# First tile's shift from eight one-column matmuls, second tile and two weight slabs loaded in two parts, one split held behind a norm's first step

## The chip, the cores and the metric

The kernel runs on one core of a Trainium2 chip (trn2). The metric is the device time of one execution in microseconds (us), the median over several executions. A profile of one further execution records every instruction of every engine: TensorE as PE (matmuls) and PEld (weight loads), VectorE as DVE, ScalarE as ACT, GpSimd as POOL, and the queue of SyncE, which issues the transfers, as SPq.

## What is computed

Two layers, each with three sub-layers over 256 tokens of width 1024 (`x`), in 32-bit floats. Every sub-layer is fed `x * (1 + scale) + shift`, and its result enters a layer norm through a gate. The nine vectors of a layer come from one conditioning vector `c`.

```python
c_act = jax.nn.silu(c)
for l in range(DEPTH):
    mod = c_act @ mod_w[l] + mod_b[l]
    sh1, sc1, g1, sh2, sc2, g2, sh3, sc3, g3 = jnp.split(mod, N_MOD, axis=-1)
    f = swiglu(modulate(x, sh1, sc1), ffn_in[l, 0], ffn_out[l, 0])
    x = deepnorm_residual(x, f, g1, ln_g[l, 0], ln_b[l, 0], 0.5)
    u = modulate(x, sh2, sc2)
    m = even_mixer(u, ...) if l % 2 == 0 else odd_mixer(u, ...)
    x = deepnorm_residual(x, m, g2, ln_g[l, 1], ln_b[l, 1])
    f = swiglu(modulate(x, sh3, sc3), ffn_in[l, 1], ffn_out[l, 1])
    x = deepnorm_residual(x, f, g3, ln_g[l, 2], ln_b[l, 2], 0.5)
```

## The kernel before, in words

Activations lie transposed: eight tiles k = 0..7 of 128 features by 256 tokens. All weights are read once, in the order in which they are used, as slabs of 1 MiB (16 blocks of 128x128, `wst`). A slab is turned, half by half, into two parts that TensorE multiplies faster than plain 32-bit data: ACT rounds it (`whi`, line 365), DVE subtracts the rounded part from the raw one (`wlo`, line 374, called the split here). A product is then three matmuls (`mm3`, lines 489 to 491): high weight with high activation, high weight with low activation, low weight with high activation. Slab 0 alone is used raw, in plain 32-bit matmuls.

The columns of `mod` are made on DVE: line 450 multiplies a 128x1024 tile of transposed `mod_w` by silu(c), spread over all partitions (`cact`), and sums each row. That gives one column (one tile k, one of the nine vectors) per instruction. For the first tile, k = 0, the two columns (shift and scale) are made from halves of 512, as soon as each half of the spread vector is there: four instructions at line 468 (`reduce_first`).

The head runs like this. SP issues, in this order, `cvec` (c and the first biases), `m0a` and `m0b` (the rows of `mod_w` for tile 0, half by half, the second with tile 0 of x), slab 0, `m1x` (the rows of tile 1 with tiles 1 to 3 of x), slab 1, the rows of tile 2, slab 2, the rows of tile 3, slab 3, `x47` (the other tiles of x), `cols`, and then slabs and rows of `mod_w` in turn. TensorE runs five warming matmuls (line 524), four matmuls that spread silu(c) over the partitions (line 556), and seven further warming matmuls. Then the first pass of the first channel mixer begins: k = 0 to 3, with eight columns j of gate and up each (line 970), sixteen products for every k from slab k. Ahead of the products of k, `first_u(k)` queues on ACT and DVE, in an order that is fixed by hand (`queue_behind`): the two reductions of k, the halving of slab k's first half (ACT 365, DVE 374), the modulated tile (`uhi` at line 649, `ut` at line 651, `ulo` at line 657), then the second half of the slab. After k = 3 the eight sums are set aside (line 986) and the next columns follow with all k, now by `mm3`.

A channel mixer ends with eight output tiles f, each the sum over 22 products (`ffn_out`). `tile_out` (line 770 for the tile `yy`, line 777 for its square) adds the residual. After f = 7, `stats` lets TensorE sum the parts that came before (line 807), multiplies ahead for the next sub-layer (lines 489 to 491 on `flat`), sums the last tile (line 816) and its square (line 817), and goes on multiplying ahead. Conversions of weights run five half slabs ahead of their use, so a split stands in DVE's queue every eight products. With `W.defer` set, `conv_to` doesn't queue a split but keeps it in `W.pending`, and `tile_out` issues it right behind the next `yy`. The kernel before does that at the end of the odd mixer only.

Of the kernel before, what the change touches and what calls it, by code (L numbers as in the profile page):

```python
# [11 lines left out]
F32 = mybir.dt.float32  # L12
F32R = mybir.dt.float32r
BF16 = mybir.dt.bfloat16
# [7 lines left out]
P = 128  # L22
# [36 lines left out]
RAWSLABS = 1  # L59
NWARM = (5, 7)  # L60

# [180 lines left out]
@with_exitstack  # L242
def trunk_kernel(ctx: ExitStack, tc: tile.TileContext, cvec, m0a, m0b, m1x, x47, pos, wst, modw, colsd,
                 rgw, wa2, outT):
# [69 lines left out]
    class Stream:  # L314
# [22 lines left out]
        def dma_to(self, n):  # L337
            while self.ndma < min(n, NSLAB):
                s = self.ndma
                self.mods_to(self.mod_target(s))  # L340
                t = T(wraw, [P, SLAB * P], tag="wraw")
                self.raw[s] = t
                self.ndma += 1
                self.last_dma = sync.dma_start(t, wst[s])
                if s == KSPLIT - 1:
                    sync.dma_start(self.xrest, x47)
                    sync.dma_start(cols, colsd)
# [60 lines left out]
        def mods_to(self, n):  # L408
            while self.nmod < n:
                if self.nmod < KSPLIT:  # L410
                    t = self.early_mod(self.nmod)
                else:
                    t = T(wraw, [P, 2, DM], tag="wraw")
                    sync.dma_start(t, modw[self.nmod])
                self.todo += [(2 * self.nmod + q, t[:, q, :], self.ndma) for q in range(2)]
                self.nmod += 1

        def begin(self, first, second):

            a, b = (t.rearrange("p j s -> p (j s)") for t in (first, second))  # L420
            HD = DM // 2
            self.m0 = [[a[:, o + v * HD:o + (v + 1) * HD] for v in range(2)] for o in (0, DM)]
            self.m0rows = a[:, :DM], a[:, DM:2 * DM + SEQ]
            o = 2 * DM + SEQ
            self.m1rows = a[:, o:o + 2 * DM + (KSPLIT - 1) * SEQ]
            pair = lambda t: t.rearrange("p (v d) -> p v d", v=2)
            self.early = [None, pair(a[:, o:o + 2 * DM])] + [pair(b[:, i * 2 * DM:(i + 1) * 2 * DM]) for i in range(2)]
            x1 = o + 2 * DM
            self.xrest = b[:, 4 * DM:4 * DM + (KD - KSPLIT) * SEQ]
            self.x = [a[:, 2 * DM:2 * DM + SEQ]] + [a[:, x1 + i * SEQ:x1 + (i + 1) * SEQ] for i in range(KSPLIT - 1)] + \  # L430
                [self.xrest[:, i * SEQ:(i + 1) * SEQ] for i in range(KD - KSPLIT)]

        def early_mod(self, n):
            if n == 0:

                for t, m in zip(self.m0rows, (m0a, m0b)):
                    sync.dma_start(t, m)
                return self.m0rows[0].rearrange("p (v d) -> p v d", v=2)
            sync.dma_start(*((self.m1rows, m1x) if n == 1 else (self.early[n], modw[n])))
            return self.early[n]  # L440

# [16 lines left out]
        def reduce_first(self):  # L458

            part = T(const, [P, 2], tag="part")  # L460
            for v in (SH, SC):
                self.modcols[(0, v)] = T(const, [P, KD], tag=f"mod0_{v}")
            del self.todo[:2]
            for h in range(2):
                for v, t, b in zip((SH, SC), self.m0[h], (shb, scb)):
                    junk = T(wk, [P, DM], BF16, tag="junk", bufs=1)
                    p = part[:, v:v + 1]
                    i = vec.tensor_tensor_reduce(junk[:, :DM // 2], t, spread[h], float(P), b[:, 0:1] if h == 0 else p, MULT,
                                                 ADD, p if h == 0 else self.modcols[(0, v)][:, 0:1])
                    queue_behind(i, self.last_reduce)  # L470
                    self.last_reduce = i

# [59 lines left out]

    chi = T(const, [P, KD], F32R, tag="chi")
    clo = T(const, [P, KD], tag="clo")
    with tc.high_priority():
        ta(chi, cT, AF.Silu)
        ta(clo, cT, AF.Silu)
        vec.tensor_tensor(clo, clo, chi.bitcast(F32), SUB)
        dhi, dlo = (T(main, [P, KD, P], F32R, tag=f"flat{q}") for q in range(2))
# [19 lines left out]
        for i, j in zip(pds[1:], pds):  # L559
            queue_behind(i, j)  # L560

    warm(NWARM[1], pds[-1])

# [50 lines left out]
    def begin(first, second):  # L614
        W.begin(first, second)
        W.dma_to(1)

        W.last_reduce = vec.tensor_scalar(scb, scb, 1.0, None, ADD)
# [313 lines left out]
    def ffn(l, i, prev):  # L932
        with tc.tile_pool(name=nm("ffn"), bufs=1) as fp:
# [77 lines left out]
            for f in range(KD):  # L1011
                ps = mmps()
                for k in range(NJ):
                    mm3(ps[:, :SEQ], W.next((("ffn_out", l, i), k, f)), (hhi[:, k, :], hlo[:, k, :]),
                        k == 0, k == NJ - 1)
# [530 lines left out]
def _lay_out(inp):  # L1546
# [50 lines left out]
    xt = f["x"][0].T.reshape(KD, P, SEQ).transpose(1, 0, 2)  # L1597
    halves = modw[0].reshape(P, 2, 2, DM // 2).transpose(2, 0, 1, 3).reshape(2, P, DM)

# [10 lines left out]
    for i, name in enumerate(("rg_wa", "rg_wx")):  # L1610
        for n in range(2 * KD):
# [4 lines left out]
            [as_cols(f["c"])] + [as_cols(f["mod_b"][0, v * DM:(v + 1) * DM]) for v in (SH, SC)], axis=1)),  # L1616
        "m0a": beside(halves[0]),
        "m0b": beside(halves[1], xt[:, 0]),
        "m1x": beside(modw[1], xt[:, 1:KSPLIT]),
        "x47": beside(xt[:, KSPLIT:]),  # L1620
# [25 lines left out]
```

## Time and profile before

| | us |
|---|---|
| median of 3 runs | 1008.31 (1007.86 to 1008.39) |
| the profiled execution | 1007.84 |
| its span, first to last instruction | 1006.1 |
| PE busy in the span | 995.9 |
| DVE busy | 878.2 |
| ACT busy | 611.7 |
| mean granted clock of TensorE, as a share of full | 0.997 |

Matmuls are pipelined, so that a busy PE is not PE at its peak; what counts is where PE stands still or waits. "Idle before" in brackets at the end of a row is the time that the engine had stood still when the instruction began, and what ended it. Weight loads (PEld) run ahead of the matmuls that they belong to, and their starts show best when PE came free.

### The profile page before, as it was taken

Reading aid. Unit: us, or ns where it says so; the run is one execution under the profiler, and the core shown is the slowest. Engines: PE = TensorE matmul, PEld = TensorE weight load, DVE = VectorE, ACT = ScalarE, POOL = GpSimd, SP = SyncE. Lnnn points to the kernel's source line nnn. Section 1 sums busy time; section 2 is a strip of 40 time slices with the busy share of each in tenths; the row PEclk is TensorE's granted clock in tenths of the full one; section 3 lists DMA queues with packets and bytes.
Section 4 is the critical chain, followed back from the end, with each engine's and each line's share of the span. In section 5 each row is a group of like instructions: output and inputs, shape, how many; then the busy total and the mean of one; then the engine's idle time right before and its main releaser. Section 6 shows DMA issues by size and latency. Waiting matters only on the chain.

```text
span 1006.1 us, 20567 instructions
## 1 busy us (share of the span) xinstructions
PE 995.9 (99%) x8354; PEld 976.0 (97%) x8354; DVE 878.2 (87%) x1511; ACT 611.7 (61%) x1033; POOL 4.6 (0%) x24
## 2 busy tenths in 40 slices
PE   9999999999999999999999999999999999999997
PEld 8999999998999999999999999999999999999996
DVE  6789999998999899999996999999788799666664
ACT  4656655578886766645554665454568767554542
POOL 0000000000000000000000000000000000000000
PEclk9999999999999999999999999999999999999998
DMA  9998698755467744799975479898743156766501
GB/s 373 421 392 325 252 365 313 296 210 219 158 244 296 297 169 171 298 374 394 342 298 221 171 267 387 326 329 333 281 168 126 50 183 240 283 217 246 190 21 42
DMA packets 36383, 258.79 MB, mean 257 GB/s; under 512 B 4160, under 2 KB 4416, under 8 KB 5312
## 3 DMA queue, kind: packets, MB, share of 16 engines
q1 hardware_dynamic: 36144, 257.09, 67.8%
q8 instruction: 65, 1.06, 0.4%
q10 hardware_dynamic: 144, 0.39, 0.1%
q14 instruction: 30, 0.25, 0.1%
HBM read 256.42 MB, written 1.05 MB: 256 GB/s over the span
## 4 chain that ended last, share of the span: by engine, by line
PE 85%; DVE 8%; ACT 3%; issue 3%; DMA 1%; SPq 0%; DVEq 0%; ACTq 0%
PE mm L491 26%; PE mm L490 25%; PE mm L489 25%; DVE wlo L374 3%; DVE junk L450 2%; DMA wraw<-wst 1%; ACT whi L365 1%; PE mm L1267 1%; PE mm L1268 1%; PE mm L1266 1%; PE ax L490 1%; PE ax L491 1%; PE ax L489 1%; PE ax L1467 0%; PE mm L1441 0%
## 5 line engine op out<-in xcount | busy, mean ns | idle before, releaser
L374 DVE TENSOR_TENSOR wlo<-wraw,whi 128x1024 fp32r<-128x1024 f32 x338 | 408.7, 1217 | 72.6 <-ACT whi L365 71.9
L365 ACT ACTIVATE whi<-wraw 128x1024 fp32r<-128x1024 f32 x338 | 354.0, 1057 | 163.1 <-PE mm L490 117.2
L491 PE MATMUL mm<-uhi,wlo 128*128 128x256 f32 x1624 | 449.1, 277 | 0.2 <-DVE wlo L374 0.2
L489 PE MATMUL mm<-uhi,whi 128*128 128x256 f32 x1624 | 449.3, 277 | 0.0
L490 PE MATMUL mm<-ulo,whi 128*128 128x256 f32 x1624 | 449.1, 277 | 0.0
L491 PEld LDWEIGHTS mm<-uhi,wlo 128*128 128x128 f32 x1624 | 304.6, 188 | 0.7 <-DVE wlo L374 0.4
L489 PEld LDWEIGHTS mm<-uhi,whi 128*128 128x128 f32 x1624 | 304.8, 188 | 0.4 <-ACT uhi L1470 0.2
L490 PEld LDWEIGHTS mm<-ulo,whi 128*128 128x128 f32 x1624 | 304.8, 188 | 0.4
L489 PE MATMUL mm<-hhi,whi 128*128 128x256 f32 x704 | 194.4, 276 | 0.0
L491 PE MATMUL mm<-hhi,wlo 128*128 128x256 f32 x704 | 194.4, 276 | 0.0
L490 PE MATMUL mm<-hlo,whi 128*128 128x256 f32 x704 | 194.4, 276 | 0.0
L450 DVE CUSTOM_DVE_ANT_0 junk<-wraw,cact,cols 128x1024 bf16<-128x1024 f32 x128 | 163.1, 1275 | 4.8 <-DMA wraw<-modw 4.5
L490 PEld LDWEIGHTS mm<-hlo,whi 128*128 128x128 f32 x704 | 132.2, 188 | 0.0
L489 PEld LDWEIGHTS mm<-hhi,whi 128*128 128x128 f32 x704 | 132.2, 188 | 0.0
L491 PEld LDWEIGHTS mm<-hhi,wlo 128*128 128x128 f32 x704 | 132.2, 188 | 0.0
L565 ACT ACTIVATE hhi<-h 128x256 fp32r<-128x256 f32 x88 | 35.8, 413 | 66.4 <-DVE h L947 66.2
L777 ACT ACTIVATE ysq<-yy 128x256 f32<-128x256 f32 x42 | 17.5, 416 | 59.9 <-DVE yy L770 59.6
L947 DVE SCALAR_TENSOR_TENSOR h<-mm,sg 128x256 f32<-128x256 f32 x75 | 30.3, 414 | 6.4 <-PE mm L491 6.4
L566 DVE TENSOR_TENSOR hlo<-h,hhi 128x256 fp32r<-128x256 f32 x88 | 35.6, 414 | 0.1
L770 DVE SCALAR_TENSOR_TENSOR yy<-mm,gate,ax 128x256 f32<-128x256 f32 x48 | 22.9, 478 | 13.8 <-PE mm L491 13.7
L511 ACT ACTIVATE sg<-mm 128x256 f32<-128x256 f32 x75 | 27.4, 367 | 6.1 <-PE mm L491 3.0
L489 PE MATMUL mm<-flat,whi 128*128 128x258 f32 x96 | 28.5, 297 | 0.0
(340 smaller groups left out, 1126.9 us busy)
## 6 DMA issues: line engine op xcount, KB each, us to landing
wraw<-wst SPq DMA_DIRECT2D x170, 1024.0 KB, 5.6
wraw<-modw SPq DMA_DIRECT2D x68, 1024.0 KB, 6.6
hhi<-modw SPq DMA_DIRECT2D x2, 1024.0 KB, 16.1
hlo<-m1x SPq DMA_DIRECT2D x1, 1408.0 KB, 9.7
wraw<-rgw SPq DMA_DIRECT2D x1, 1024.0 KB, 5.5
hlo<-m0b SPq DMA_DIRECT2D x1, 640.0 KB, 4.7
hlo<-m0a SPq DMA_DIRECT2D x1, 512.0 KB, 3.6
hhi<-x SPq DMA_DIRECT2D x1, 512.0 KB, 20.9
```

Of the source, the lines that this page charges most:

```text
L365: ia = act.activation(hi, raw, AF.Copy)
L374: i = vec.tensor_tensor(lo, raw, hi.bitcast(F32), SUB)
L450: i = vec.tensor_tensor_reduce(junk, t, cact, 1.0, bias, MULT, ADD, self.modcols[(l, v)][:, j:j + 1])
L489: pe.matmul(ps, hi, mh, start=start, stop=False, skip_group_check=shared)
L490: pe.matmul(ps, hi, ml, start=False, stop=False, skip_group_check=shared)
L491: W.last_product = pe.matmul(ps, lo, mh, start=False, stop=stop, skip_group_check=shared)
L511: i = act.activation(out, in_, func, **kw)
L565: act.activation(hi, src, AF.Copy)
L566: return vec.tensor_tensor(lo, src, hi.bitcast(F32), SUB)
L770: i = vec.scalar_tensor_tensor(y, ps, self.gate[:, f:f + 1], ax[:, f, :], MULT, ADD)
L777: act.activation(ysq, y, AF.Square)
L947: vec.scalar_tensor_tensor(h, pu, bu, sg, ADD, MULT)
```

## The change

For tile 0, the shift isn't reduced on DVE any more. Its 128 columns of `mod_w` are loaded as eight blocks of 128x128, with as many bytes as before, and TensorE multiplies each by one column of silu(c) (a new tile `cs`), summing in PSUM; DVE then adds the bias. Line 468's four instructions become two, for the scale. The eight matmuls stand behind the spreading ones, and four warming matmuls follow instead of seven. `m1x` becomes two transfers: the first row set with tile 1 of x, then the second row set with tiles 2 and 3. Slabs 1 and 2 are each loaded by two transfers, half by half. At the end of the first channel mixer, from the twelfth product of the last output tile on, `W.defer` is set.

```diff
-NWARM = (5, 7)
+NWARM = (5, 4)
...
-                self.last_dma = sync.dma_start(t, wst[s])
+
+                parts = 2 if RAWSLABS <= s < RAWSLABS + 2 else 1
+                for q in range(parts):
+                    n1 = SLAB * P // parts
+                    self.last_dma = sync.dma_start(t[:, q * n1:(q + 1) * n1], wst[s][:, q * n1:(q + 1) * n1])
...
-            self.m0 = [[a[:, o + v * HD:o + (v + 1) * HD] for v in range(2)] for o in (0, DM)]
+
+            self.m0 = a[:, :HD], a[:, DM:DM + HD]
+            self.m0shift = [a[:, o + k * P:o + (k + 1) * P] for o in (HD, DM + HD) for k in range(KD // 2)]
...
-            self.m1rows = a[:, o:o + 2 * DM + (KSPLIT - 1) * SEQ]
+            o2 = o + DM + SEQ
+            end = o2 + DM + (KSPLIT - 2) * SEQ
+
+            self.m1rows = a[:, o:o2], a[:, o2:end]
...
-            sync.dma_start(*((self.m1rows, m1x) if n == 1 else (self.early[n], modw[n])))
-            return self.early[n]
+                return [None, None]
+            if n == 1:
+                for t, m in zip(self.m1rows, (m1a, m1b)):
+                    sync.dma_start(t, m)
+                return self.early[1]
+            sync.dma_start(self.early[n], modw[n])
+            return [self.early[n][:, q, :] for q in range(2)]
...
-            for h in range(2):
-                for v, t, b in zip((SH, SC), self.m0[h], (shb, scb)):
-                    junk = T(wk, [P, DM], BF16, tag="junk", bufs=1)
-                    p = part[:, v:v + 1]
-                    i = vec.tensor_tensor_reduce(junk[:, :DM // 2], t, spread[h], float(P), b[:, 0:1] if h == 0 else p, MULT,
-                                                 ADD, p if h == 0 else self.modcols[(0, v)][:, 0:1])
-                    queue_behind(i, self.last_reduce)
-                    self.last_reduce = i
+            scale, shift = (self.modcols[(0, v)][:, 0:1] for v in (SC, SH))
+            for h, t in enumerate(self.m0):
+                junk = T(wk, [P, DM], BF16, tag="junk", bufs=1)
+                i = vec.tensor_tensor_reduce(junk[:, :DM // 2], t, spread[h], float(P), part if h else scb[:, 0:1], MULT, ADD,
+                                             scale if h else part)
+                queue_behind(i, self.last_reduce)
+                self.last_reduce = i
+            i = vec.tensor_tensor(shift, self.shift0, shb[:, 0:1], ADD)
+            queue_behind(i, self.last_reduce)
+            self.last_reduce = i
...
+    cs = T(const, [P, KD], tag="cs")
...
-        ta(clo, cT, AF.Silu)
-        vec.tensor_tensor(clo, clo, chi.bitcast(F32), SUB)
+        ta(cs, cT, AF.Silu)
+        vec.tensor_tensor(clo, cs, chi.bitcast(F32), SUB)
...
-    warm(NWARM[1], pds[-1])
...
         W.dma_to(1)
+
+        sp = mmps()
+        W.shift0 = sp[:, 0:1]
+        prods = [pe.matmul(sp[:, 0:1], w, cs[:, k:k + 1], start=k == 0, stop=k == KD - 1) for k, w in enumerate(W.m0shift)]
+        after = pds[-1]
+        for i in prods:
+            queue_behind(i, after)
+            after = i
+        warm(NWARM[1], after)
...
                 for k in range(NJ):
+                    if l == 0 and i == 0 and f == KD - 1 and k == NJ // 2:
+
+                        W.defer = True
```

## Rows read from the trace of the kernel before

**Rows 1.** Page, busy time of each engine over the span.
```profile
PE 995.9 (99%) x8354; PEld 976.0 (97%) x8354; DVE 878.2 (87%) x1511; ACT 611.7 (61%) x1033; POOL 4.6 (0%) x24
```
**Rows 2.** Waits of the whole span: engine, line, releaser, us in total, times, longest.
```profile
PEld mm L970 <- ACT uhi L649: 1.2, 3, 0.5
```
**Rows 3.** Chain that ended last, 0 to 30 us: start, us, what.
```profile
3.19 11.62 DMA wraw<-wst
```
**Rows 4.** Timeline, TensorE in the head: start, us, engine, line, operation, count, idle before.
```profile
5.87 2.52 PE L524 MATMUL mm<-ones_dm 128*128 128x128 f32 x14
9.17 5.45 PE L970 MATMUL mm<-ut,wraw 128*128 128x256 f32 x24 [0.78 <-ACT ut L651]
16.43 1.00 PEld L970 LDWEIGHTS mm<-uhi,whi 128*128 128x128 f32 x8 [0.49 <-ACT uhi L649]
...
28.17 0.99 PEld L970 LDWEIGHTS mm<-uhi,whi 128*128 128x128 f32 x8 [0.34 <-ACT uhi L649]
33.63 0.19 PEld L489 LDWEIGHTS mm<-uhi,whi 128*128 128x128 f32 x1
```
**Rows 5.** Timeline, ACT and DVE in the head.
```profile
4.72 0.17 DVE L618 TENSOR_SCALAR cfirst<-cfirst 128x8 f32<-128x8 f32 x1
8.52 0.60 ACT L651 ACTIVATE ut<-hlo,mod,mod 128x256 f32<-128x256 f32 x1 [4.15 <-DVE mod L468]
12.48 1.28 DVE L450 CUSTOM_DVE_ANT_0 junk<-hlo,cact,cfirst 128x1024 bf16<-128x1024 f32 x1 [2.46 <-DMA hlo<-m1x]
14.83 1.06 ACT L365 ACTIVATE whi<-wraw 128x1024 fp32r<-128x1024 f32 x1 [3.99 <-DMA wraw<-wst]
26.11 1.06 ACT L365 ACTIVATE whi<-wraw 128x1024 fp32r<-128x1024 f32 x1 [2.11 <-DMA wraw<-wst]
27.52 0.60 ACT L649 ACTIVATE uhi<-hlo,mod,mod 128x256 fp32r<-128x256 f32 x1 [0.35 <-DVE mod L450]
```
**Rows 6.** Timeline, SP's queue: rows of tile 3, slab 3 and `x47` issued.
```profile
4.86 0.51 SPq L439 DMA_DIRECT2D hhi<-modw  x1
5.42 0.44 SPq L344 DMA_DIRECT2D wraw<-wst  x1
6.46 0.33 SPq L346 DMA_DIRECT2D hhi<-x  x1
```
**Rows 7.** DMA issues, the same three: KB, us from issue to landing.
```profile
hhi<-modw SPq DMA_DIRECT2D x1, 1024.0 KB, 18.9
wraw<-wst SPq DMA_DIRECT2D x1, 1024.0 KB, 20.7
hhi<-x SPq DMA_DIRECT2D x1, 512.0 KB, 20.9
```
**Rows 8.** Waits of SP's queue, 0 to 60 us.
```profile
SPq L346 <- DMA hlo<-m0b: 0.6, 1, 0.6
```
**Rows 9.** Windows: us; busy PE, PEld, DVE, ACT, POOL; granted clock; DMA share; GB/s.
```profile
5.00:10.00 5.00, 4.22 (x21) 3.74 (x20) 3.42 (x9) 1.45 (x4) 0.00 (x0) 1.00 1.03 431
```
**Rows 10.** Chain that ended last: 16 plain 32-bit products of 64 columns (two entries each).
```profile
275.02 3.52 PE mm L1216 x32
```
**Rows 11.** Timeline, first norm: DVE and TensorE.
```profile
191.93 1.22 DVE L374 TENSOR_TENSOR wlo<-wraw,whi 128x1024 fp32r<-128x1024 f32 x1
192.18 0.54 PEld L807 LDWEIGHTS ax<-early,ones_d 128*128 128x128 f32 x4
193.06 0.48 DVE L770 SCALAR_TENSOR_TENSOR yy<-mm,gate,ax 128x256 f32<-128x256 f32 x1
194.43 0.19 PEld L489 LDWEIGHTS mm<-flat,whi 128*128 128x128 f32 x1
194.49 0.48 DVE L741 SCALAR_TENSOR_TENSOR flat<-yy,A,flat 128x256 fp32r<-128x256 f32 x1 [0.94 <-ACT flat L740]
```
**Rows 12.** Timeline, norm after the second layer's first mixer: TensorE.
```profile
737.29 0.54 PEld L807 LDWEIGHTS ax<-early,ones_d 128*128 128x128 f32 x4
738.97 0.19 PEld L489 LDWEIGHTS mm<-flat,whi 128*128 128x128 f32 x1
```

More of the change, by code (lines that the diff above doesn't have):

```diff
@@ L242, in trunk_kernel @@
 @with_exitstack
-def trunk_kernel(ctx: ExitStack, tc: tile.TileContext, cvec, m0a, m0b, m1x, x47, pos, wst, modw, colsd,
+def trunk_kernel(ctx: ExitStack, tc: tile.TileContext, cvec, m0a, m0b, m1a, m1b, x47, pos, wst, modw, colsd,
                  rgw, wa2, outT):
@@ L414, in mods_to @@
                     sync.dma_start(t, modw[self.nmod])
-                self.todo += [(2 * self.nmod + q, t[:, q, :], self.ndma) for q in range(2)]
+                    t = [t[:, q, :] for q in range(2)]
+                self.todo += [(2 * self.nmod + q, t[q], self.ndma) for q in range(2)]
                 self.nmod += 1
@@ L421, in begin @@
             HD = DM // 2
-            self.m0 = [[a[:, o + v * HD:o + (v + 1) * HD] for v in range(2)] for o in (0, DM)]
+            self.m0 = a[:, :HD], a[:, DM:DM + HD]
+            self.m0shift = [a[:, o + k * P:o + (k + 1) * P] for o in (HD, DM + HD) for k in range(KD // 2)]
             self.m0rows = a[:, :DM], a[:, DM:2 * DM + SEQ]
             o = 2 * DM + SEQ
-            self.m1rows = a[:, o:o + 2 * DM + (KSPLIT - 1) * SEQ]
+            o2 = o + DM + SEQ
+            end = o2 + DM + (KSPLIT - 2) * SEQ
+            self.m1rows = a[:, o:o2], a[:, o2:end]
             pair = lambda t: t.rearrange("p (v d) -> p v d", v=2)
-            self.early = [None, pair(a[:, o:o + 2 * DM])] + [pair(b[:, i * 2 * DM:(i + 1) * 2 * DM]) for i in range(2)]
-            x1 = o + 2 * DM
+            self.early = [None, (a[:, o:o + DM], a[:, o2:o2 + DM])] + [pair(b[:, i * 2 * DM:(i + 1) * 2 * DM]) for i in range(2)]
             self.xrest = b[:, 4 * DM:4 * DM + (KD - KSPLIT) * SEQ]
-            self.x = [a[:, 2 * DM:2 * DM + SEQ]] + [a[:, x1 + i * SEQ:x1 + (i + 1) * SEQ] for i in range(KSPLIT - 1)] + \
+            self.x = [a[:, 2 * DM:2 * DM + SEQ], a[:, o + DM:o2]] + \
+                [a[:, o2 + DM + i * SEQ:o2 + DM + (i + 1) * SEQ] for i in range(KSPLIT - 2)] + \
                 [self.xrest[:, i * SEQ:(i + 1) * SEQ] for i in range(KD - KSPLIT)]
@@ L437, in early_mod @@
                     sync.dma_start(t, m)
-                return self.m0rows[0].rearrange("p (v d) -> p v d", v=2)
-            sync.dma_start(*((self.m1rows, m1x) if n == 1 else (self.early[n], modw[n])))
-            return self.early[n]
+                return [None, None]
[5 more added lines that the diff above has]
+            return [self.early[n][:, q, :] for q in range(2)]
         def reduce(self):
@@ L458, in reduce_first @@
         def reduce_first(self):
-            part = T(const, [P, 2], tag="part")
+            part = T(const, [P, 1], tag="part")
             for v in (SH, SC):
@@ L1597, in _lay_out @@
     xt = f["x"][0].T.reshape(KD, P, SEQ).transpose(1, 0, 2)
-    halves = modw[0].reshape(P, 2, 2, DM // 2).transpose(2, 0, 1, 3).reshape(2, P, DM)
+    HD = DM // 2
+    shift0 = f["mod_w"][0][:, SH * DM:SH * DM + P].reshape(KD, P, P).transpose(1, 0, 2).reshape(P, DM)
     def beside(*a):
@@ L1616, in _lay_out @@
             [as_cols(f["c"])] + [as_cols(f["mod_b"][0, v * DM:(v + 1) * DM]) for v in (SH, SC)], axis=1)),
-        "m0a": beside(halves[0]),
-        "m0b": beside(halves[1], xt[:, 0]),
-        "m1x": beside(modw[1], xt[:, 1:KSPLIT]),
+        "m0a": beside(modw[0][:, SC, :HD], shift0[:, :HD]),
+        "m0b": beside(modw[0][:, SC, HD:], shift0[:, HD:], xt[:, 0]),
+        "m1a": beside(modw[1][:, 0], xt[:, 1]),
+        "m1b": beside(modw[1][:, 1], xt[:, 2:KSPLIT]),
         "x47": beside(xt[:, KSPLIT:]),
```

## The prediction

> **What bounds the kernel now.** I read the page first: TensorE is busy for 99% of the span [rows 1], so the end moves only where TensorE stands still. The list of waits then names the places that the change could touch: three waits of the first pass, 1.2 us together, for the modulated tile `uhi` [rows 2]. The timeline shows where they lie, and what a norm waits for.
>
> In the head, TensorE's first real product begins at 9.17, and the sixteen products of k = 1, 2, 3 follow. Their starts at 16.43 and 28.17 stood idle for ACT's `uhi` [rows 4]. From 28.17 to 33.63 there is no wait inside, so sixteen halved products cost TensorE 5.46 us. For k = 0 the products are plain: 24 entries in 5.45 us, less some 0.17 of overlap at the end, make 0.22 us each, and 32 of them some 7.0 us [rows 4].
>
> What `uhi` waits for is told by ACT and DVE. ACT's conversion of slab 1 waited for the slab until 14.83, that of slab 3 until 26.11; the first reduction of tile 1 waited for `m1x` until 12.48 [rows 5]. The chain of the first 30 us is, for its first 15 us, one transfer, slab 1's [rows 3]. So the head is bound by arrival, and the DMA engines are full there (share 1.03, 431 GB/s [rows 9]): what lands can be used in smaller pieces, but not brought sooner as a whole.
>
> At the first norm, DVE begins a split at 191.93; `yy` stands behind it and starts at 193.06, although TensorE had begun loading for the sums, which follow its last product, at 192.18. TensorE is back on product work at 194.43 [rows 11].
>
> **The change part by part.** *First tile.* Two of four DVE reductions go. Before, their end let ACT start `ut` at 8.52, and with 0.60 us of that, TensorE began at 9.17 [rows 4, 5]. Now the shift comes from eight plain products, sixteen entries, behind the spreading ones at 5.87. The trace has no one-column product. The nearest rows: 64 columns take 3.52/32 = 0.11 us an entry [rows 10]; the warming ones in the same place take 2.52/14 = 0.18 [rows 4]. So the products take 1.8 to 2.9 us and end at 7.6 to 8.8; fewer columns may cut it further, but the weights must be loaded all the same, so I set no lower end than 0.11. I take 8.5, nearer to the warming rows, which stand in the same microseconds. With 0.17 for the addition [rows 5], some 0.1 of signals and `ut`'s 0.65 to the first product, TensorE starts at 9.4 to 9.5: 0.3 later, not earlier (bounds 9.0, where the earlier end leads after slab 0 is in, and 9.8). The four warming matmuls (eight entries, 0.9 to 1.4 us) stand ahead of the first product in TensorE's queue and end at 9.4 to 9.9, and may push it as far as 9.9. DVE is freed for 0.75 us or so, with nothing waiting there.
>
> *Tile 1 and slabs 1 and 2 in two parts.* Bytes and order stay, so a first half lands half a transfer earlier. From slab 3 to `x47`, half a slab took 6.46 + 20.9 - 5.42 - 20.7 = 1.24 us [rows 6, 7]; so slab 1's first half lands at about 13.6 instead of 14.8, and tile 1's first rows about 1.9 before 12.4. Both reductions of tile 1 are then done by 13.8, ACT has the half slab converted by 14.7 and `uhi` 0.6 later, before TensorE leaves k = 0 at 9.5 + 7.0 = 16.5. That start no longer waits. Tile 2 follows. In the trace its products began at about 22.3 (16.43 + 5.46, and a third of the 1.2 us of waiting [rows 2]); its reductions stand behind tile 1's splits on DVE and move up by the same microsecond, so it can begin at 21.3. TensorE arrives at 16.5 + 5.46 = 21.96. No wait.
>
> Tile 3 is what is late next. Slab 3 isn't split, and lands at 26.1 as before; ACT's fixed order puts `uhi` behind that conversion: 26.11 + 1.06 = 27.15 or so, with the start overlapping, and 0.65 more (27.52 to 28.17) to the product: 27.8 [rows 4, 5]. The reductions must also be done: the rows of tile 3 land at 4.86 + 18.9 = 23.8 [rows 6, 7], and two reductions of 1.3 from there end at 26.4, ahead of 27.15 instead of behind the conversion at 27.5. TensorE itself arrives at 21.96 + 5.46 = 27.4. So k = 3 begins at 27.8 instead of 28.17: **0.4 us gained**, whatever the first tile does, as long as TensorE's first product starts before 27.8 - 2 x 5.46 - 7.0 = 9.9. The bounds: 0 if TensorE starts k = 0 at 10.2 or slab 3 lands 0.4 later, 0.8 if slab 3 lands early (then TensorE's own 27.4 decides).
>
> The queues that the parts pass: SP issues three transfers more. `x47` was held until `m0b` had landed, eight transfers before it [rows 8], so I read a limit of eight in flight. Three more in the row put slab 3's issue back from 5.42 to where the first part of tile 1 lands, about 10.5. There are then seven transfers, 4.75 MiB, ahead of it, some 11 us of work at the full rate, so the engines don't run dry. `x47` and `cols` go behind as before.
>
> A rule of the Trainium skill speaks against this part. "DMA: Bandwidth & Descriptors" (section Measured) wants transfers of 1 MiB or more, and its anatomy section gives a fixed cost of about 2 us for each. By that, three more transfers would put slab 3 off by up to 6 us. The row above disagrees: the half-size `x47` landed 1.24 us behind the slab ahead of it, with no fixed cost.
>
> *The held split.* The last output tile's conversions come at every eighth product; the channel mixer has 352 products of the first kind and 22 for each output, so the last one begins at 506, `W.defer` is set at 517, and one boundary, 520, lies behind it before 528. So exactly the split of 191.93 is held. Its price is read from a norm of the same kind in which nothing stood in DVE's way: there TensorE took from 737.29 to 738.97, 1.68 us, between the same two steps that took 192.18 to 194.43, 2.25 us, here [rows 11, 12]. **0.57 us gained.** The split (1.22) now lies between `yy` and the steps on DVE that follow the sums. In the trace DVE stood idle for 0.94 us there, waiting for ACT, until 194.49 [rows 11]; the split fills that and puts off what follows by 0.1 to 0.3, against 0.6 by which `yy` is earlier. The weights that it makes are wanted some 3 us later. Bounds: 0 (some other step of DVE takes its place) and 0.8.
>
> **Does the gain last?** Behind 33.6 the same steps follow from TensorE's progress, and every transfer issued there is released by a buffer that DVE frees. DVE is busy for 87% of the span [rows 1], but its work starts from buffers that TensorE frees, so it moves with it. I count nothing for that and nothing gained.
>
> **The sum.** 0.4 + 0.57 = 0.97 us off the profiled execution's 1007.84: 1006.87. The median of the runs stands 0.47 above that execution, so the forecast for the median is 1007.3, which is 0.1% less than 1008.31. A difference of 0.2%, 2.0 us, is about what a measurement can tell from no change.
>
> **The rivals.** *Only the norm gains* (chance 0.2): slab 3 lands 0.4 later, or the first product comes after 9.9 because of the warming matmuls. 1008.31 - 0.57 = 1007.7. *Slab 3 lands earlier* by a microsecond, as transfers in parts are spread better (0.12): 0.8 + 0.6, 1006.9 and down to 1006.5 with both upper bounds. *The hold does nothing* (0.06): DVE has something else ahead of `yy`: 1007.9.
>
> *TensorE's clock* (0.06, slower): the granted clock reads 1.00, the level of 2.4 GHz, in 5 to 10 us [rows 9], but the entries tell another story, 0.18 us for 128 columns in the warming matmuls against 0.11 later for 64 [rows 4, 10], so TensorE seems to be at the lower level until the last of them. Sixteen entries of one column in their place keep the array nearly empty. If the higher level comes later for that, plain products of k = 0 cost 0.44 instead of 0.22. From 1.4 us of such delay on, six or seven entries, the gains are gone; with half of k = 0, 3.5 us more, k = 3 begins at 9.5 + 10.5 + 10.9 = 30.9, 2.7 later: 1008.31 + 2.7 - 0.57 = 1010.4; with all of it 1014. For it: nothing but these eight products changes there. Against it: loads and matmuls still follow without a gap. "TensorE: Matmul & The Clock Gate" of the Trainium skill (Part 1) has the same: throttled is the default, and activity releases it. By that rule, if one-column products count for little, the loss is as above; no run shows it yet.
>
> *The order of work elsewhere moves* (0.06, mostly slower): the added tile and the hold shift what the planner places, and DVE, with 13% of its time free [rows 1], delays a norm: a stall of the 0.6 us of the first norm at three of the other five, 1.7 us, or as much gained. *More transfers cost* (0.02): slab 3 some 6 us later gives 1013.
>
> **The numbers.** The forecast case has 0.48. The range 1006.4 to 1008.7 holds it, the only-the-norm case, the early slab and the useless hold; what is left out is the clock, the transfers and part of the order. Faster by over 0.2%: 0.06; within: 0.87; slower: 0.07.
>
> **What would show it.** Right: the reduction of tile 1 begins near 10.5, ACT's first conversion near 13.6, slab 2's a microsecond earlier than before and slab 3's still near 26.1; `uhi` waits vanish for k = 1 and 2 and one near 0.4 us is left at k = 3, whose products begin near 27.8; `yy` at the first norm starts ahead of the split, and the norm takes TensorE 1.7 us. Wrong: a first product after 9.9, entries of 0.44 us in k = 0, a conversion of slab 3 far from 26.1, or a norm that still takes 2.2.

## The result and the profile after

| kernel | median, us | lowest to highest | profiled execution | its span |
|---|---|---|---|---|
| before | 1008.11 | 1007.86 to 1008.88 | 1007.84 | 1006.1 |
| changed | 1011.04 | 1009.65 to 1011.59 | 1010.67 | 1009.0 |

Both medians are of nine executions. The change makes the kernel slower by 2.9 us: ratio 1.0027, 95% interval 1.0017 to 1.0036. The forecast was 1007.3, in a range from 1006.4 to 1008.7.

The first fence is the changed kernel's timeline in the head, TensorE's matmuls (PE) and loads (PEld): start, us, engine, line, operation, shapes, count. It answers [rows 4]. L635 are the eight products, L540 the warming matmuls, L994 the products of the first pass.

```profile
5.91 3.41 PE L635 MATMUL mm<-cs,hlo 128*128 128x1 f32 x16
9.18 2.06 PE L540 MATMUL mm<-ones_dm 128*128 128x128 f32 x8
11.02 6.39 PE L994 MATMUL mm<-ut,wraw 128*128 128x256 f32 x24
18.77 1.10 PEld L994 LDWEIGHTS mm<-uhi,whi 128*128 128x128 f32 x8
24.32 0.98 PEld L994 LDWEIGHTS mm<-uhi,whi 128*128 128x128 f32 x8
29.77 0.98 PEld L994 LDWEIGHTS mm<-uhi,whi 128*128 128x128 f32 x8
35.20 0.19 PEld L505 LDWEIGHTS mm<-uhi,whi 128*128 128x128 f32 x1
```

The sixteen entries of the products take 3.41 us, 0.21 each, and the eight warming entries behind them another 1.84. The first real product begins at 11.02 (before: 9.17), k = 1, 2, 3 at 18.77, 24.32, 29.77. No start carries a wait any more, since TensorE now comes later than what it waited for; k = 3 and the pass behind it (35.20) are 1.6 us later than in [rows 4].

The next fence shows weight loads by microsecond: window, length, PEld busy with the loads in it (x), granted clock, DMA share, GB/s.

```profile
10.00:11.00 1.00, 1.00 (x6) 1.00 1.04 436
11.00:12.00 1.00, 0.82 (x4) 1.00 0.99 369
12.00:13.00 1.00, 0.82 (x3) 1.00 1.00 250
13.00:14.00 1.00, 0.83 (x5) 1.00 0.88 250
14.00:15.00 1.00, 0.88 (x5) 1.00 1.11 455
```

From 11 to 13 us a microsecond holds 3 or 4 loads, later 5: five entries of k = 0 take 0.43 us, those behind 13.16 take 0.215. That is the ratio of TensorE's two levels, 1.2 and 2.4 GHz. The clock column reads 1.00 all the way, but the trace's records of the granted clock begin only at 13.14 (7.54 in the kernel before), just where the entries halve; ahead of its first record the column shows nothing else. The same windows hold a second finding, the fall to 250 GB/s from 12 to 14 us.

ACT and DVE in the head, answering [rows 5]; the bracket is the idle time ahead and what ended it.

```profile
9.55 0.60 ACT L675 ACTIVATE ut<-hlo,mod,mod 128x256 f32<-128x256 f32 x1 [5.14 <-DVE mod L485]
11.60 1.28 DVE L464 CUSTOM_DVE_ANT_0 junk<-hlo,cact,cfirst 128x1024 bf16<-128x1024 f32 x1 [0.55 <-ACT cact L680]
14.43 1.06 ACT L369 ACTIVATE whi<-wraw 128x1024 fp32r<-128x1024 f32 x1 [2.56 <-DMA wraw<-wst]
27.07 1.06 ACT L369 ACTIVATE whi<-wraw 128x1024 fp32r<-128x1024 f32 x1 [3.48 <-DMA wraw<-wst]
```

`ut` is done at 10.15, the warming matmuls end at 11.0: they, not ACT, set the first product. Slab 1's first half is converted from 14.43 (14.83 before), slab 3 only from 27.07 (26.11 before).

Two stalls of TensorE are new, both far from the edited places. The list of waits (engine, line, releaser, us in total, times, longest), where the kernel before has 0.4 us in one wait:

```profile
PEld mm L507 <- DVE wlo L378: 2.0, 3, 1.2
```

and the two on the timeline:

```profile
120.95 0.19 PEld L507 LDWEIGHTS mm<-uhi,wlo 128*128 128x128 f32 x1 [0.48 <-DVE wlo L378]
157.74 0.19 PEld L507 LDWEIGHTS mm<-hhi,wlo 128*128 128x128 f32 x1 [1.15 <-DVE wlo L378]
```

The first norm, answering [rows 11]:

```profile
195.65 0.55 PEld L831 LDWEIGHTS ax<-early,ones_d 128*128 128x128 f32 x4
195.97 0.48 DVE L794 SCALAR_TENSOR_TENSOR yy<-mm,gate,ax 128x256 f32<-128x256 f32 x1 [2.04 <-PE mm L507]
196.37 1.22 DVE L378 TENSOR_TENSOR wlo<-wraw,whi 128x1024 fp32r<-128x1024 f32 x1
197.34 0.19 PEld L505 LDWEIGHTS mm<-flat,whi 128*128 128x128 f32 x1
```

`yy` starts ahead of the split, and the norm takes 197.34 - 195.65 = 1.69 us of TensorE, against 2.25. The ledger of the two spans: +1.60 in the head, +0.48 and +1.15 at the stalls, -0.56 at the norm, together +2.67 of 2.9. The brackets are a little less than what is lost: the same loads come 0.55 and 1.24 us later at the two stalls than in the kernel before, which brings the ledger to +2.83.

### The profile page after: what moved, and what is told of

Its sections match the earlier page's. It is cut to its first block, busy times and chain, and to the rows that moved or that the text cites. A ratio compares the mean times of both kernels' runs of the same rounds, so it can differ in the third digit from the quotient of the medians.

```text
span 1009.0 us, 20591 instructions
## 1 busy us (share of the span) xinstructions
PE 999.2 (99%) x8364; PEld 979.8 (97%) x8364; DVE 877.3 (87%) x1508; ACT 612.1 (61%) x1033; POOL 4.8 (0%) x24
## 3 DMA queue, kind: packets, MB, share of 16 engines
HBM read 256.42 MB, written 1.05 MB: 255 GB/s over the span
## 4 chain that ended last, share of the span: by engine, by line
PE 88%; DVE 8%; ACT 2%; issue 2%; DMA 0%; DVEq 0%; ACTq 0%
PE mm L507 26%; PE mm L506 26%; PE mm L505 26%; DVE wlo L378 2%; DVE junk L464 2%; PE mm L994 2%; PE mm L1294 1%; PE mm L1295 1%; PE mm L1293 1%; DVE flat L1016 0%; DVE h L971 0%; PE ax L994 0%; PE ax L505 0%; PE ax L1494 0%; PE ax L506 0%
```

## The experiments

The theories. **Level:** one-column entries leave TensorE at its lower level, so that products, warming matmuls and part of k = 0 go at half speed. Its rival: the number of entries costs. **Order:** the kernel's planner put the steps of DVE and ACT into another order, which makes the two stalls. Its rival: everything is late because the head is. **Parts:** the halved loads bring slab 3 later. **Hold:** it gains what was predicted. All times below are medians, each against executions of the kernel before on the same chip.

| kernel | us | before | difference | ratio, 95% interval |
|---|---|---|---|---|
| old first tile (parts, hold) | 1007.70 | 1008.44 | -0.74 | 0.9993 [0.9985, 1.0002] |
| old first tile, new order | 1009.58 | 1008.44 | +1.14 | 1.0011 [1.0002, 1.0020] |
| changed, old order | 1008.88 | 1008.44 | +0.44 | 1.0003 [0.9995, 1.0012] |
| changed, old order, products 128 wide | 1007.96 | 1008.44 | -0.48 | 0.9995 [0.9986, 1.0004] |
| hold alone | 1008.10 | 1008.66 | -0.56 | 0.9994 [0.9985, 1.0002] |
| parts alone | 1008.43 | 1008.66 | -0.23 | 0.9996 [0.9987, 1.0005] |
| before, warming one column wide | 1009.71 | 1008.66 | +1.05 | 1.0010 [1.0001, 1.0019] |
| products alone | 1011.20 | 1008.66 | +2.54 | 1.0021 [1.0012, 1.0030] |
| changed, again | 1010.91 | 1008.56 | +2.35 | 1.0021 [1.0012, 1.0030] |
| hold, tile 1 in parts | 1008.04 | 1008.56 | -0.52 | 0.9995 [0.9986, 1.0004] |
| hold, slabs in parts | 1007.80 | 1008.56 | -0.76 | 0.9993 [0.9984, 1.0002] |
| old tile, new order, one step back | 1009.06 | 1008.49 | +0.57 | 1.0006 [0.9997, 1.0015] |

An interval reaches some 0.9 us to either side. Clear of no change are the old first tile with the new order, the one-column warming, the products alone and the changed kernel; each of the other differences, taken by itself, could be none.

### The old first tile in the changed kernel

```diff
-NWARM = (5, 4)
+NWARM = (5, 7)
...
-            self.m0 = a[:, :HD], a[:, DM:DM + HD]
+            self.m0 = [[a[:, o + v * HD:o + (v + 1) * HD] for v in range(2)] for o in (0, DM)]
...
-        prods = [pe.matmul(sp[:, 0:1], w, cs[:, k:k + 1], start=k == 0, stop=k == KD - 1) for k, w in enumerate(W.m0shift)]
...
-        warm(NWARM[1], after)
```

with `reduce_first` and the layout of `m0a`, `m0b` as before.

> The changed kernel with its first tile put back as it was (four reductions on DVE, seven warming matmuls, no products); the loads in two parts and the held split stay. The steps on DVE, ACT and TensorE then stand in the order of the kernel before. If the first tile's products cost the time (late first product, and the new order of steps behind it), both new stalls near 121 and 158 us are gone, the first product begins near 9.2, k = 3 between 27.8 (slab 3 lands at 26.1) and 28.8 (at 27.05, as in the changed kernel), and the norm keeps its gain of 0.5: 1007.2 to 1008.2 where the kernel before has 1008.1. If the loads in parts cost by themselves, k = 3 begins at 28.8 or later and the time is 1008.5 or more. If the hold makes the stalls, they stay: 1009 or more.

Measured -0.74: both stalls are gone, slab 3 is converted from 27.21, k = 3 begins at 28.81 behind a wait of 0.9, and the norm takes 1.68. So the first tile's products, with the order that comes with them, carry the whole loss, and the rest of the change is at most a small gain. Its highest time, 1008.08, is below the lowest of the kernel before there, 1008.19, though the interval still touches 1.

### The order of steps, with the old head and with the new one

Compared step by step in the traces, the parts leave the order on DVE, ACT and TensorE as it was. The hold puts the split behind `yy` and moves four more steps on DVE and one on ACT, between 212 and 217 us. The products move far more: at least 36 of DVE's 1511 steps, 14 of ACT's 1033 and 12 of TensorE's matmuls change places, all between 43 and 184 us. The program's planner made both orders; why the products change its choice isn't shown. The two kernels carry the order of the other, written as a chain of ordering edges without waits:

```diff
+    ORDER = {
+        "DVE": (...), "ACT": (...), "PE": (...),
+    }
+    made = {str(i.name): i for i in nc.all_instructions()}
+    for names in ORDER.values():
+        for a, b in zip(names, names[1:]):
+            tc.add_manual_dep(made[f"I-{b}"], f"I-{a}", mybir.DependencyInfo(
+                mybir.DependencyClass.NoSync, mybir.DependencyReason.DATA), reason="order")
```

> As the run with the old first tile, but the steps on DVE, ACT and TensorE between about 40 and 230 us are put, by ordering alone, into the order that they have in the changed kernel. The head is the old one, so its 1.6 us are not lost. If the new order makes the two stalls (0.4 and 1.0 us), they come back here near 119 and 156 us and the time is 1.4 us above the run with the old tile: 1008.6 to 1009.6. If the late head makes them (DVE and ACT 2 us behind), they don't come, and the time is that of the run with the old tile within 0.3 us.

> The changed kernel whole, products of one column and all, but with the steps on DVE, ACT and TensorE between about 40 and 230 us put, by ordering alone, into the order of the kernel before. If the new order makes the two stalls, they are gone and only the head's 1.6 us less the norm's 0.5 are left: 1009.2 to 1009.6, against 1011.0 of the changed kernel. If the late head makes the stalls, it stays at 1010.6 to 1011.2.

| | old order | new order |
|---|---|---|
| old first tile | -0.74 | +1.14 |
| products | +0.44 | +2.35 (the changed kernel again) |

The order costs 1.88 with the old head and 1.91 with the new, the products by themselves 1.18 and 1.21. The stalls follow the order and not the late head: with the old head and the new order TensorE waits again; with the new head and the old order both stalls are gone. The third expectation named 1009.2 to 1009.6; 1008.88 is lower, but its executions reach from 1007.70 to 1009.97.

What the order does is read on DVE ahead of the stall near 156 us. Timeline, DVE and the load in question, first the old order (old first tile):

```profile
147.29 1.22 DVE L378 TENSOR_TENSOR wlo<-wraw,whi 128x1024 fp32r<-128x1024 f32 x1
...
151.30 1.28 DVE L463 CUSTOM_DVE_ANT_0 junk<-wraw,cact,cols 128x1024 bf16<-128x1024 f32 x1
...
153.25 1.28 DVE L463 CUSTOM_DVE_ANT_0 junk<-wraw,cact,cols 128x1024 bf16<-128x1024 f32 x1
...
154.53 1.22 DVE L378 TENSOR_TENSOR wlo<-wraw,whi 128x1024 fp32r<-128x1024 f32 x1
...
154.96 0.19 PEld L504 LDWEIGHTS mm<-hhi,wlo 128*128 128x128 f32 x1
```

then the new one, with the old first tile too:

```profile
150.78 1.27 DVE L463 CUSTOM_DVE_ANT_0 junk<-wraw,cact,cols 128x1024 bf16<-128x1024 f32 x1
...
152.45 1.27 DVE L463 CUSTOM_DVE_ANT_0 junk<-wraw,cact,cols 128x1024 bf16<-128x1024 f32 x1
...
154.40 1.27 DVE L463 CUSTOM_DVE_ANT_0 junk<-wraw,cact,cols 128x1024 bf16<-128x1024 f32 x1
...
155.68 1.21 DVE L378 TENSOR_TENSOR wlo<-wraw,whi 128x1024 fp32r<-128x1024 f32 x1
...
156.95 0.19 PEld L504 LDWEIGHTS mm<-hhi,wlo 128*128 128x128 f32 x1 [1.15 <-DVE wlo L378]
```

A split serves eight of TensorE's loads, so that counting the loads of `wlo` tells which split each of them needs. The load at 156.95 in the new order, and the same load at 154.96 in the old one, need the 51st split. In the old order that is the one at 147.29, done more than six microseconds ahead of its use; the one at 154.53 is the split after it. In the new order the 51st split is the one at 155.68: the three reductions shown are ahead of it, all of which stand behind it in the old order, and TensorE waits 1.15 for it. The stall near 120 us is smaller and of the same kind: its split starts at 118.89 with the new order, at 117.50 with the old one, in part because one step of `h` (0.41 us) stands ahead of it; what makes up the rest was not taken apart.

### One step put back

In the new order with the old first tile, the third reduction goes behind the split (numbers are those of the instructions):

```diff
-        "DVE": (... 1788, 1830, 1789, 1970, 1790 ...
+        "DVE": (... 1788, 1789, 1970, 1830, 1790 ...
```

> The run with the old tile and the new order, with a single exchange in that order: the third of the three reductions that stand on DVE ahead of the split near 155.7 us goes behind that split, as it does in the kernel before. If these 1.28 us of a reduction ahead of the split are what TensorE waited for there (1.2 us), that stall is gone, the other near 119.5 us (0.5) stays, the time falls by about 1.2 us and lies 0 to 0.3 below or above the kernel before (0.74 below with the old order, and 0.5 of the stall near 119.5 on top). If the split is late for another reason (a late slab, or everything on DVE being late), the stall stays or comes back at the next split, and the time stays 1.1 us above the kernel before.

Against the kernel before, the difference fell from +1.14 to +0.57, by half of what was expected. The waits of TensorE's loads for `wlo`, over the span: us in total, times, longest. New order, then with the step back:

```profile
PEld mm L504 <- DVE wlo L378: 2.0, 3, 1.1
```

```profile
PEld mm L504 <- DVE wlo L378: 1.0, 3, 0.5
```

The long stall is gone, but this split and the next two, at 154.23, 157.15 and 160.28, now end only 0.06 us ahead of the loads that need them (155.50, 158.42 and 161.55). These loads lose 0.13, 0.16 and 0.36 us, 0.65 together, where 1.23 was lost before: the reduction that went behind the first split stands ahead of the second. So the reduction explains half of the stall. The other half is that the new order makes the 51st split eight microseconds later than the old one, and with it the lead that the next splits had (1.9 and 2.2 us in the old order) is gone. That moving this one split back would undo the whole stall was not run; the old order as a whole does undo it.

### Products 128 columns wide

```diff
-        prods = [pe.matmul(sp[:, 0:1], w, cs[:, k:k + 1], start=k == 0, stop=k == KD - 1) for k, w in enumerate(W.m0shift)]
+        prods = [pe.matmul(sp[:, :128], w, cs[:, k:k + 1].broadcast_to([P, 128]), start=k == 0, stop=k == KD - 1) for k, w in enumerate(W.m0shift)]
```

The chain of ordering edges comes with it.

> The changed kernel with each of its eight products 128 columns wide (the column of c read 128 times over; column 0 is used), in the same 16 entries, and with the steps behind the head in the order of the kernel before. If the one-column entries keep TensorE at its lower level, entries fall from 0.21 to 0.11 us near 7.5 us already, as in the kernel before: products and warming matmuls end near 9.2 instead of 11.0, no entry of k = 0 takes 0.43, k = 2 and k = 3 wait for slabs again, and the time is that of the run with the old tile within 0.4: 1007.2 to 1008.4. If it is the number of entries that costs, the first product still begins near 11.0 and k = 3 a microsecond or two late: 1008.8 to 1009.6.

The timeline of its head:

```profile
5.99 3.31 PE L635 MATMUL mm<-cs,hlo 128*128 128x128 f32 x16
9.13 1.05 PE L540 MATMUL mm<-ones_dm 128*128 128x128 f32 x8
10.18 5.45 PE L994 MATMUL mm<-ut,wraw 128*128 128x256 f32 x24
```

With the order the same, it is 0.92 faster than the one-column kernel, about as much as an interval reaches; the next experiment tries the same in a single edit. An entry of 128 columns is no slower than one of a single column (0.21 us each until 8.8), and from there on entries take 0.11: the warming ones 1.05 instead of 2.06, and k = 0 has none of 0.43. So the loss goes with the width of the entries and not with their number. Two points of the expectation failed: the first product came at 10.18, not near 9.2, since the higher level came at 8.8 here, and k = 2 did not wait. Against the old first tile the wide products are no gain: -0.48 and -0.74 with the same parts and hold.

### Warming matmuls one column wide, in the kernel before

```diff
-    def warm(n, after=None):
+    def warm(count, after=None, n=P):
...
-        for _ in range(n):
-            i = pe.matmul(ps[:, :P], ones_dm, ones_dm, start=True, stop=True)
+        for _ in range(count):
+            i = pe.matmul(ps[:, :n], ones_dm, ones_dm[:, :n], start=True, stop=True)
...
-    warm(NWARM[1], pds[-1])
+    warm(NWARM[1], pds[-1], 1)
```

> The kernel before with one edit: the seven warming matmuls behind the spreading ones are one column wide instead of 128, in the same 14 entries; the order of all steps is unchanged. If one-column entries keep TensorE at its lower level, entries of k = 0 take 0.43 instead of 0.22 us until some 12 or 13 us, as in the changed kernel: from 9.2 to 13.1 that is nine entries for eighteen, 1.9 us, of which the waits at k = 1, 2, 3 (0.4, 0.3, 0.3) take up to 1.0: the time is 0.9 to 1.9 us above the kernel before. If the number of entries alone counts, nothing changes: within 0.2.

No step changes its place, no entry is added, and the time rises by 1.05. The timeline, against [rows 4]:

```profile
5.85 2.98 PE L524 MATMUL mm<-ones_dm 128*128 128x1 f32 x14
9.52 7.48 PE L970 MATMUL mm<-ut,wraw 128*128 128x256 f32 x24 [0.69 <-DMA wraw<-wst]
```

All fourteen entries stay at 0.21 us, and the 24 of k = 0 take 7.48 instead of 5.45. k = 3 begins at 29.76, 0.9 to 1.6 us later than in the kernels with whole slabs and full-width entries (28.17, 28.68 and 28.84).

### Products alone

The changed kernel with its loads whole again and without the hold: of the three parts of the change only the products are left.

> The kernel before with the first tile's shift by eight one-column products alone (loads whole, no hold). The steps then stand in the order of the changed kernel. If late clock and new order are what costs, both show here too: entries of 0.43 us until about 13, k = 3 about 1.4 us later than 28.17, the two stalls of 0.4 and 1.0 us, in all 2.5 to 3.3 us above the kernel before. If they need the loads in parts as well, the time is at most 1 us above it.

+2.54, with the new order's two stalls, which so need neither the parts nor the hold. Its profiled execution shows the level itself. Timeline and windows, as above:

```profile
5.81 2.10 PE L624 MATMUL mm<-cs,hlo 128*128 128x1 f32 x16
9.44 6.94 PE L983 MATMUL mm<-ut,wraw 128*128 128x256 f32 x24 [0.53 <-DMA wraw<-wst]
```

```profile
8.00:9.00 1.00, 0.71 (x7) 1.00 1.06 446
9.00:10.00 1.00, 0.51 (x3) 0.55 1.00 428
10.00:11.00 1.00, 0.82 (x3) 0.50 1.00 428
11.00:12.00 1.00, 0.82 (x3) 0.50 0.98 411
12.00:13.00 1.00, 0.79 (x5) 0.74 1.00 426
13.00:14.00 1.00, 0.90 (x5) 1.00 0.99 418
```

Here TensorE was at the higher level from 5.7 us: the products' entries take 0.11. Behind them the granted clock falls to 0.50 at 9.1 and comes back at 12.5, and between the two k = 0 has three loads a microsecond. TensorE also stood still for 0.53 us just ahead of its first product; but with the old first tile in the changed kernel it stood still for 2.66 us there, at the higher level since 4.6 us, and kept it. This was the fastest execution, 1009.88, of a median of 1011.20; its k = 3 begins at 28.73, so that the head lost 0.56 us here and not the 1.4 that was expected. No slower execution was profiled.

### Hold alone, parts alone, and each half of the parts

> The kernel before with the held split alone: the three lines that set W.defer ahead of the last conversion before the first norm. If the hold does what the prediction says, TensorE takes 1.7 us instead of 2.25 between its load for the sums and its next products at the first norm, nothing else moves, and the time is 0.5 to 0.6 us below the kernel before. If some other step takes the place of the split ahead of yy, it is the same within 0.1. If putting the split off delays the steps on DVE that follow the sums, the stall comes back later and the time is equal or up to 0.5 above.

Measured -0.56 (the interval touches 1). The first norm, from the load for the sums to the next products; L741 is the step on DVE behind the held split:

```profile
192.86 0.54 PEld L807 LDWEIGHTS ax<-early,ones_d 128*128 128x128 f32 x4
...
194.54 0.19 PEld L489 LDWEIGHTS mm<-flat,whi 128*128 128x128 f32 x1
194.71 0.85 DVE L741 SCALAR_TENSOR_TENSOR flat<-yy,A,flat 128x256 fp32r<-128x256 f32 x1
```

1.68 us, for 2.25 in [rows 11].

> The kernel before with the loads in two parts alone (tile 1's rows, slabs 1 and 2): no products, no hold. The prediction gave it 0.4 us less, with slab 3 landing at 26.1 and k = 3 beginning at 27.8. In the kernels with the parts measured so far, slab 3 landed at 27.05 to 27.7 and k = 3 began at 28.8 and 29.0 with the old tile: then it costs 0.6 to 0.8 us, and the time is that much above the kernel before. Between the two (no change) if slab 3's landing varies from one execution to the next by that much whatever the kernel.

-0.23: no loss of 0.6 to 0.8, and no gain that can be told from none. ACT's conversions of slab 1's first half and of slab 3:

```profile
14.98 1.06 ACT L369 ACTIVATE whi<-wraw 128x1024 fp32r<-128x1024 f32 x1 [3.84 <-DMA wraw<-wst]
...
27.18 1.06 ACT L369 ACTIVATE whi<-wraw 128x1024 fp32r<-128x1024 f32 x1 [3.03 <-DMA wraw<-wst]
```

The first half of slab 1 isn't there earlier than the whole slab was (14.83 in [rows 5]), slab 3 is later, and TensorE still waits for `uhi` at all three starts: 0.20 us at k = 1, 0.34 at k = 2, 0.60 at k = 3, which begins at 28.78. To find what delays slab 3, the two halves of the edit were taken apart, each with the hold:

```diff
                 self.ndma += 1
-                self.last_dma = sync.dma_start(t, wst[s])
+
+                parts = 2 if RAWSLABS <= s < RAWSLABS + 2 else 1
+                for q in range(parts):
+                    n1 = SLAB * P // parts
+                    self.last_dma = sync.dma_start(t[:, q * n1:(q + 1) * n1], wst[s][:, q * n1:(q + 1) * n1])
```

stands in the one of the following two that halves the slabs, and not in the other, which has tile 1's rows in two transfers (`m1a`, `m1b`).

> The kernel before with the held split and with tile 1's rows alone in two parts: slabs 1 and 2 whole, old first tile. If the slow packets near 12 to 14 us (263 to 300 ns for 4 KB, against 159 ns later) come from slab 1 being halved, they are gone, slab 3 lands at 26.1 to 26.3, k = 3 begins by 28.8, and the time is 0.5 to 0.9 us below the kernel before. If they come from tile 1's rows in two parts, the packets of slab 1 are slow here too (over 320 ns for 8 KB, against 311 in the kernel before), slab 3 lands at 27 or later.

> The kernel before with the held split and with slabs 1 and 2 alone in two parts: tile 1's rows whole, old first tile. If the slow packets near 12 to 14 us come from slab 1 being halved, they are here too, slab 3 lands at 27.0 to 27.7, k = 3 begins at 28.7 or later, and the time lies 0.3 to 0.8 us below the kernel before, by the hold. If tile 1's rows in two parts make them, they are gone and slab 3 lands by 26.4.

Windows (us, length, granted clock, DMA share, GB/s) and, on the timeline, slab 3's conversion, tile 1 in parts:

```profile
12.00:13.00 1.00, 1.00 1.01 424
13.00:14.00 1.00, 1.00 1.01 426
```

```profile
26.32 1.06 ACT L365 ACTIVATE whi<-wraw 128x1024 fp32r<-128x1024 f32 x1 [1.81 <-DMA wraw<-wst]
```

and slabs in parts:

```profile
12.00:13.00 1.00, 1.00 0.90 253
13.00:14.00 1.00, 1.00 0.88 225
```

```profile
27.11 1.06 ACT L369 ACTIVATE whi<-wraw 128x1024 fp32r<-128x1024 f32 x1 [2.79 <-DMA wraw<-wst]
```

It is the halving of slab 1: the slow packets are its own. For two microseconds the engines are busy and move half as much: packets of 4 KB take 235 to 255 ns there, later ones of the same size 159 to 162. What is lost, about (425 - 239) x 2 = 370 KB, is 0.9 us at 425 GB/s, and slab 3 comes that much later. Why slab 1's first half is slow and slab 2's halves are not stays open. The time doesn't follow: with slabs in parts -0.76, with tile 1 alone -0.52, the hold alone -0.56. k = 3 begins at 28.71, 28.68 and 28.84, so that no loss is seen from the later slab 3.

### The changed kernel again

> The changed kernel itself once more, beside the same runs of the kernel before as the two kernels with it, so that the terms can be added up: 2.5 to 3.3 us above the kernel before, by 2.5 for the products alone (entries of 0.43 us early on, and the order of steps with its two stalls) less 0.56 for the hold, with the parts between -0.2 and +0.6. Its times should spread over 1.5 to 2.5 us, as those of the other kernels with one-column entries did (2.3, 2.7, 2.1), against 0.4 to 0.7 for those without, if the moment at which the higher level comes differs from one execution to the next.

+2.35, inside the interval of the first measurement. It is under the range of the expectation, but that range wasn't the sum of the terms beside it, 2.5 - 0.56 and -0.2 to +0.6, which is 1.7 to 2.5 and holds it. The terms as they were measured in a row: old first tile -0.74, order +1.88, products +1.18, sum +2.32. Added up from the single edits, products alone, hold and parts, it would be 2.54 - 0.56 - 0.23 = 1.75; so the single terms add up to within some 0.6 us, no better.

## Why the prediction was wrong, step by step

**First tile: wrong in size, and through that in kind.** This step of the prediction failed. It priced an entry of the products by 2.52/14 = 0.18 us, the mean of the warming entries, and set 2.9 us as the upper end. That mean is a mix: in the kernel before the entries take 0.21 until 7.5 us and 0.11 behind it. The price at the lower level is 0.21, and 3.41 us were needed. The same slip hid in the warming matmuls, 0.9 to 1.4 us predicted and 1.84 taken, so that the first product stood behind both, at 11.02 and not at 9.4 to 9.9.

**TensorE's clock: the right rival with too small a chance, 0.06.** Its mechanism is what happened; five entries of k = 0, not half of it, ran at 0.43, some 1.1 us in all. The argument against it, that loads and matmuls follow without a gap, carried no weight: they follow without a gap in the narrow warming too. In the profiled executions the trace's first record of the higher level lies between 4.6 and 9.5 us for the kernel before and all kernels with full-width entries and the old first tile, at 8.8 for the wide products, and between 13.1 and 13.9 for four of the five executions with one-column entries; the fifth is the products alone, with its fall. With full-width entries that range cost nothing: in none of these executions did the first real product begin ahead of that record. "TensorE: Matmul & The Clock Gate" of the Trainium skill (Part 1) says that throttled is the default and that activity releases it. The traces agree in that the entries ahead of the first record take twice as long as those behind it (0.21 and 0.11 us in the kernel before).

**Parts: wrong, a term that wasn't there.** The step took it that a first half lands half a transfer, 1.24 us, earlier, slab 1's at 13.6, and that slab 3 lands at 26.1 as before. Neither came. ACT's conversion of slab 1 begins at 14.4 to 15.5 in the nine kernels with halved slabs and at 14.8 to 15.5 in the five without; that of slab 2 at 19.5 to 20.6 and at 19.8 to 20.5, not a microsecond earlier; slab 3's at 26.9 to 27.7 and at 26.1 to 26.3. The slow packets of slab 1's first half use up the microsecond that the halving was to gain, and slab 3 gets it as a delay. That the waits of k = 1 and k = 2 vanish in the changed kernel looks like the prediction, but comes from TensorE being late: they vanish with whole slabs too, in the one-column warming and in the products alone, and with the parts alone 0.20 and 0.34 us of them are left. Of the gain of 0.4 there is 0.23 or nothing. The base was a sample besides: the profiled execution of the kernel before has k = 3 at 28.17, two kernels with whole slabs and the old first tile have 28.68 and 28.84. The loss of up to 6 us, estimated from "DMA: Bandwidth & Descriptors" of the Trainium skill (section Measured, and the section on the anatomy of one transfer), isn't seen in any run. Both sections give their figures for transfers issued from GpSimd; here SP issues them.

**Hold: right.** 2.25 became 1.68 on TensorE, as predicted, and the time fell by 0.56 for 0.57, though its interval doesn't exclude no change. The step on DVE that was to be put off a little, but by less than `yy` gains (L741), stood 2.31 us behind TensorE's load for the sums in [rows 11], and stands 1.85 behind it with the hold alone (194.71 - 192.86).

**"I count nothing for that": wrong, the largest term.** The step let everything behind 33.6 us move along with TensorE. The order of steps is not fixed in this kernel: the products permute it up to 184 us, at a price of 1.9 us. The rival on order had the sign and nearly the size, 1.7 us, but named the added tile and the hold as the cause and the norms as the place, and had a chance of 0.06; that the size agrees is luck. It came with the products, and two splits, not norms, were late.

**The sum.** Of the two gains, 0.97 together, -0.74 was measured, most of it the hold. What turned it was +1.2 for the level and the longer products, and +1.9 for the order, both caused by the eight products and both in the list of rivals as separate, rare cases.

## What to carry to other kernels

Before work is moved to TensorE in a head, look at which level the entries of its neighbours run: a mean over a row that crosses the change of level prices neither, and filler of one column does not do what filler of full width does. Where a planner orders the steps, compare the orders before and after any edit: a local change can permute work a hundred microseconds away, and a kernel that has been tuned in one order can lose more there than the edit is worth. When a stall is read on a timeline, find out first which step the waiting one needs, by counting: the nearest one ahead of it can be another. A landing read in one execution is a sample; halving a transfer need not bring its first half earlier, and is not neutral for those behind it.

## What was not expected of the hardware

- A one-column plain entry takes as long as one of 128 columns at either level: 0.21 us in the changed kernel (3.41/16) and in the wide products until 8.8, 0.11 for the products alone at the higher level and for the warming matmuls behind the wide products.
- Sixteen one-column entries, with eight of full width and a pause of 0.53 us behind them, were followed by a fall of the granted clock to 0.50, from 9.1 to 12.5 us, although the level had been up (products alone).
- With one-column entries ahead of the first product a kernel's executions spread over 1.7 to 2.7 us (changed, old order, narrow warming, products alone); without them over 0.4 to 1.2.
- 4 KB packets of the first half of slab 1 moved at some 240 GB/s for 2 us with the engines busy, those of slab 2 at the full rate (422 to 426 GB/s at 18 to 20 us with the slabs in parts).
